# Placing the split weights at thirteen small distances inside their buffers, with fourteen activation slots in place of fifteen

## The chip, the core and the metric

The kernel runs on one core of one Trainium2 chip. The metric is the device time of one execution in microseconds (us). Two runs of the kernel before took 3163.54 and 3163.57 us; their median is 3163.56 us.

## The reference, cut to what matters

Two transformer-like blocks work one after the other on 256 tokens of width 2048, all in float32. Nearly all the arithmetic is a chain of matrix products with large weights, and the rest (norms, two kinds of attention in the first block; a state space branch "s5", a gated linear attention "gla" and a differential attention "diff" in the second) hangs between them:

```python
proj = h @ w_in[i]                                   # first block, 10240 columns
merged = (jax.nn.sigmoid(gate_sb) * (y_sb @ w_sb_out[i])
          + jax.nn.sigmoid(gate_ca) * (y_ca @ w_ca_out[i]))
x = x + merged @ w_mix_out[i]
g_ff, u_ff = jnp.split(h @ w_ffn_in[i], 2, axis=-1)
x = x + (jax.nn.silu(g_ff) * u_ff) @ w_ffn_out[i]
...
proj = hn @ w_in[l]                                  # second block
y_a = s5_branch(u_ssm, ...)
y_b = gla_branch(q_gla, k_gla, v_gla, ...)
y_c = diff_attn_branch(q_diff, k_diff, v_diff, ...)
h = h + merged.astype(h.dtype) @ w_out[l]
h = h + conv_gated_mlp(rmsnorm_2(h, norm_ffn_w[l]), ffn_w_up[l], ...)
```

## The kernel before, in words

**Products in parts.** Each float32 operand is split into a high part (rounded to the type float32r) and a low part (the rest), and a product is the sum of high x high, high x low and low x high. Activations lie in "slots" `s` as blocks of 128 rows (the contraction) by 512 numbers: 256 high parts, then 256 low parts. Weights come as tiles `raw` of 128x1024 ("halves"), loaded by SyncE (L460); ScalarE makes the high part `wh` (L467, `high`) and VectorE the low part `wl` (L477, `low`).

**Jobs.** The list of jobs is walked by `stream`, half by half. There are three kinds. In an AS job (100 of them) the weights are the moving operand: 128x512 of `wh` or `wl` stream past a 128x128 block of activations that was loaded as the stationary operand (L561, L562, L563). In a WS job (123 of them) it is the other way round: a 128x128 block of `wh` or `wl` is the stationary operand, and 512 columns of activations stream past the high block (L527), 256 past the low block (L531); a job is 32 such pairs in four halves of eight. One job is of a third kind, W4. Each job adds up in one of two PSUM buffers `acc`, and its "evac" generator empties `acc` when the last half is through.

**What sets the order.** Everything is issued in the order in which `stream` writes it, each engine running its own instructions in that order and waiting on semaphores. Before the matmuls of half i, the high split of half i+4 and the low split of half i+3 are issued; there are four `raw`, five `wh` and four `wl` buffers. After each half `tick()` advances every waiting generator by one step, and so heads, norms and evacuations are woven between the halves: a step's results have one half's time to become ready. A generator that wants a slot (`gslot`) and finds none free yields, and tries again at the next tick. A job whose `acc` buffer is still held by the job two before it forces ticks without matmuls in between (`self.tick(must=True)`), and so do `drain` and a half whose activations are not ready.

**Slots.** There are `NSLOT = 15` slots of 8192 bytes per partition; they hold activations, values, keys, a head's working space and more. The second block's heads take them in the stretch of the jobs `w_vd`, `w_u`, `w_qkd`: there `slotfree` is empty at many ticks. A gla head (`gla_head`) takes a slot `s` and then a slot `s3` for its running state: VectorE copies the first step (L1117) and adds the next six (L313), and TensorE reads them (L1130, L1134); `head_norm` follows (square on ScalarE at L310, a sum on TensorE at L1382). The evac of a `w_qkd` job (`ws_keep`, `ws_sum`) takes a slot for every four jobs and fills it from `acc` (copy on ScalarE L442, add on VectorE L443).

**Addresses.** In the built program every slot and every `raw`, `wh` and `wl` buffer starts at a multiple of 128 bytes within the partition, and every block of 128 or 512 numbers of them that TensorE reads too. The tile `big`, which is transposed at L346, lies 64 bytes past such a multiple.

Of the kernel before, what the change touches and what calls it, by code (L numbers as in the profile page):

```python
# [10 lines left out]
F32R = mybir.dt.float32r  # L11
# [12 lines left out]
CA = 4  # L24
SA = 3
COOL = 1
RAWB = 4


# [23 lines left out]
def _as(w):  # L53

    K, N = w.shape
    if K % 256:
        w = np.concatenate([w, np.zeros((256 - K % 256, N), w.dtype)], axis=0)
        K = w.shape[0]
    return np.ascontiguousarray(
        w.reshape(K // 256, 2, 128, N // 512, 512).transpose(3, 0, 2, 1, 4).reshape(-1, 128, 1024))  # L60

# [122 lines left out]


class Build:
    NSLOT = 15

    def __init__(self, tc, d, out, es):
        self.tc, self.nc, self.d, self.out = tc, tc.nc, d, out  # L190
        pool = lambda name, bufs, **kw: es.enter_context(tc.tile_pool(name=name, bufs=bufs, **kw))
        self.slotp, self.one = pool("slots", 1), pool("one", 1)
        self.rawp, self.whp, self.wlp = pool("raw", RAWB), pool("wh", CA + 1), pool("wl", SA + 1)
        self.ev = pool("ev", 2)
# [3 lines left out]
        self.psfree, self.cooling, self.ticks = [0, 1, 2, 3], [], 0  # L198
        self.slotfree = list(range(self.NSLOT))
        self.gens, self.lanes, self.nm = [], {}, 0  # L200
# [44 lines left out]
    def unbank(self, b):  # L245
        self.cooling.append((self.ticks + COOL, b[1]))

# [201 lines left out]
    def stream(self, jobs):  # L449
        nc = self.nc  # L450
        halves = [(j, i, ks) for j in jobs for i, ks in j.halves]
        N = len(halves)
        raws, spl = {}, {}
        width = lambda j, ks: {"AS": 512 * len(ks), "WS": 1024, "W4": 512}[j.kind]

        def load(i):
            j, idx, ks = halves[i]
            n = width(j, ks)
            r = self.rawp.tile([128, 1024], F32, tag="raw", name=self.name("raw"))
            nc.sync.dma_start(out=r[:, :n], in_=self.d[j.w][idx][:, :n])  # L460
            raws[i] = r

        def high(i):
            j, idx, ks = halves[i]
            n = width(j, ks)
            wh = self.whp.tile([128, 1024], F32R, tag="wh", name=self.name("wh"))
            nc.scalar.copy(wh[:, :n] if j.kind != "W4" else wh[:, :n].bitcast(F32), raws[i][:, :n])  # L467
            spl[i] = wh

        def low(i):  # L470
            j, idx, ks = halves[i]
            n = width(j, ks)
            r, wh = raws.pop(i), spl[i]
            wl = None
            if j.kind != "W4":
                wl = self.wlp.tile([128, 1024], F32R, tag="wl", name=self.name("wl"))
                nc.vector.tensor_sub(wl[:, :n], r[:, :n], wh[:, :n].bitcast(F32))  # L477
            spl[i] = (wh, wl)
            if i + RAWB < N:
                load(i + RAWB)  # L480

        ahead = self.at_start(load)
        for i in range(CA):
            next(ahead)
            high(i)
            if i < SA:
                low(i)
        self.add(ahead)
        last, prev, acc = None, None, None
        for i, (j, idx, ks) in enumerate(halves):  # L490
            if i + CA < N:
                high(i + CA)
            if i + SA < N:
                low(i + SA)
            if j is not last:
                if j.before is not None:
                    j.before()
                while prev is not None and not prev.free:
                    self.tick(must=True)
                prev, last = last, j  # L500
                acc = self.accp.tile([128, 2, 512], F32, tag="acc", name=self.name("acc"))
            for k in ks:
                while k not in j.acts.ready:
                    self.tick(must=True)
            first, end = j.halves[0][1][0], j.halves[-1][1][-1]
            if j.by_m is not None:

                for m in range(2):
                    for q, (_, _, kq) in enumerate(halves[i:]):
                        self.mm_as(j.acts, kq, *spl[i + q], acc, (m,), first, end)  # L510
                    j.by_m(m, acc)
                break
            wh, wl = spl.pop(i)
            if j.kind == "AS":
                self.mm_as(j.acts, ks, wh, wl, acc, (0, 1), first, end, low_last=i == 0)
            elif j.kind == "W4":

                for k in range(16):
                    p = slice(32 * (k % 4), 32 * (k % 4) + 32)
                    nc.tensor.matmul(acc[p, 0, :], lhsT=wh[:, 32 * k:32 * k + 32].bitcast(F32),  # L520
                                     rhs=j.acts.at(k).bitcast(F32), start=k < 4, stop=k >= 12)
            else:
                for kk, k in enumerate(ks):
                    x = j.acts.at(k)
                    for f in range(2):
                        s = slice((kk * 2 + f) * 128, (kk * 2 + f) * 128 + 128)
                        hi = lambda: nc.tensor.matmul(  # L527
                            acc[:, f, :], lhsT=wh[:, s], rhs=x, start=k == first, stop=k == end)
                        if k == first:
                            hi()  # L530
                        nc.tensor.matmul(acc[:, f, 256:512], lhsT=wl[:, s], rhs=x[:, 0:256], start=False, stop=False)  # L531
                        if k != first:
                            hi()
            if i + 1 == N or halves[i + 1][0] is not j:
                self.add(j.evac(acc, lambda j=j: setattr(j, "free", True)), front=True)
            self.tick()
        while self.gens:
            self.tick(must=True)
# [63 lines left out]
    def first(self):  # L602
# [6 lines left out]
        def start(load):  # L609
# [4 lines left out]
            def load_xt(g):  # L614
                nc.sync.dma_start(out=xs[g // 4][0][:, (g % 4) * 2:(g % 4) * 2 + 2], in_=d["xt"][:, 2 * g:2 * g + 2])

            for g in range(RAWB):
                load_xt(g)
                load(g)
            for k in range(16):  # L620
                if k % 2 == 0 and k // 2 + RAWB < 8:
                    load_xt(k // 2 + RAWB)
                if k == 8:
# [1146 lines left out]
```

## Time and profile before

| | |
|---|---|
| median of the two runs | 3163.56 us |
| the profiled execution's own time | 3164.05 us |
| its span | 3162.2 us |
| TensorE matmul busy | 3143.5 us, 16909 instructions |
| TensorE weight load busy | 2669.4 us |
| VectorE busy | 1993.3 us |
| ScalarE busy | 1553.2 us |
| granted TensorE clock, mean | 0.999 |

The page names TensorE's matmuls PE and its weight loads PEld, VectorE DVE, ScalarE ACT, GpSimd POOL and SyncE SP. A group's line has the line of the kernel, the engine, the operation, output<-inputs, the shape and the count; behind the first bar the busy time in us and the mean duration of one in ns; behind the second the idle time of that engine just before these instructions and what ended it. Matmuls are pipelined, so a matmul of 398 ns may start 227 ns after the one before it: what a matmul costs in a dense row is the distance from start to start, which the timeline gives (its columns are start in us, duration in us, engine, line, operation).

### The profile page before, as it was taken

The numbers are of one execution on the slowest core, as the hardware profiler recorded it, in microseconds if no ns is written. First come the engines' busy times: TensorE is split into PE (matmuls) and PEld (weight loads), VectorE is DVE, ScalarE is ACT, GpSimd is POOL, SyncE is SP. The second block draws the span as 40 slices with busy tenths as digits, with TensorE's granted clock in tenths as the row PEclk, the third lists the DMA queues.
The fourth block names the chain that finished last, engine by engine and source line by source line (L and its number), as shares of the span: only waits on it lengthen the run. The fifth ranks groups of instructions, "written<-read, shape, count | busy, mean of one in ns | idle before, by whom it ended". The sixth has DMA issues, their size and how long they took to land.

```text
span 3162.2 us, 43735 instructions
## 1 busy us (share of the span) xinstructions
PE 3143.5 (99%) x16909; PEld 2669.4 (84%) x16909; DVE 1993.3 (63%) x2593; ACT 1553.2 (49%) x2035; POOL 72.5 (2%) x158
## 2 busy tenths in 40 slices
PE   8999999999999999999999999999999999999998
PEld 7888888888888888888888888888888888888887
DVE  5656445557576676566655667945555766757666
ACT  6544444455444454456544454434445644545545
POOL 0000000000001000000000001000000000000000
PEclk9999999999999999999999999999999999999999
DMA  7455555555667666555654565655555565565555
GB/s 263 169 179 167 187 193 187 187 185 187 212 222 246 244 223 240 183 176 197 212 177 159 170 215 193 213 186 199 199 187 186 181 195 187 186 198 183 191 187 166
DMA packets 172640, 617.90 MB, mean 195 GB/s; under 512 B 23553, under 2 KB 23969, under 8 KB 169233
## 3 DMA queue, kind: packets, MB, share of 16 engines
q1 hardware_dynamic: 164992, 577.49, 55.1%
q0 software_dynamic: 7440, 37.64, 3.5%
q8 instruction: 132, 2.16, 0.3%
q14 instruction: 76, 0.61, 0.1%
HBM read 599.74 MB, written 14.25 MB: 194 GB/s over the span
## 4 chain that ended last, share of the span: by engine, by line
PE 99%; ACT 0%; DMA 0%; DVE 0%; DVEq 0%; issue 0%; SPq 0%; ACTq 0%
PE acc L527 29%; PE acc L561 17%; PE acc L563 17%; PE acc L562 17%; PE acc L531 15%; PE p L346 1%; PE p L1675 0%; PE p L1134 0%; PE p L1715 0%; PE p L908 0%; PE p L910 0%; PE p L909 0%; PE p L1718 0%; PE p L1111 0%; PE p L1130 0%; PE p L1709 0%
## 5 line engine op out<-in xcount | busy, mean ns | idle before, releaser
L477 DVE TENSOR_TENSOR wl<-raw,wh 128x1024 fp32r<-128x1024 f32 x1088 | 1320.2, 1220 | 649.9 <-PE acc L562 428.8
L467 ACT CAST wh<-raw 128x1024 fp32r<-128x1024 f32 x1088 | 1139.5, 1050 | 1092.5 <-PE acc L563 657.2
L527 PE MATMUL acc<-s,wh 128*128 128x512 f32 x3936 | 1385.2, 398 | 0.0
L531 PE MATMUL acc<-s,wl 128*128 128x256 f32 x3936 | 1090.7, 282 | 0.0
L561 PE MATMUL acc<-wh,s 128*128 128x512 f32 x2372 | 933.3, 393 | 0.8 <-DVE big L1353 0.8
L563 PE MATMUL acc<-wh,s 128*128 128x512 f32 x2372 | 925.0, 390 | 0.0
L562 PE MATMUL acc<-wl,s 128*128 128x512 f32 x2372 | 924.5, 390 | 0.0
L527 PEld LDWEIGHTS acc<-s,wh 128*128 128x128 f32 x3936 | 735.6, 188 | 165.0
L531 PEld LDWEIGHTS acc<-s,wl 128*128 128x128 f32 x3936 | 744.6, 189 | 11.0 <-issue 1.0
L561 PEld LDWEIGHTS acc<-wh,s 128*128 128x128 f32 x2372 | 446.0, 188 | 92.6 <-issue 1.7
L563 PEld LDWEIGHTS acc<-wh,s 128*128 128x128 f32 x2372 | 445.6, 188 | 92.9
L562 PEld LDWEIGHTS acc<-wl,s 128*128 128x128 f32 x2372 | 446.1, 188 | 91.0 <-issue 0.5
L443 DVE TENSOR_TENSOR s<-acc,s 128x512 f32<-128x512 f32 (+1 forms) x120 | 82.7, 690 | 273.9 <-ACT s L442 273.9
L442 ACT COPY s<-acc 128x512 f32<-128x512 f32 (+1 forms) x120 | 70.1, 584 | 196.6 <-PE acc L527 194.6
L310 ACT ACTIVATE s<-s 128x256 f32<-128x256 f32 (+4 forms) x175 | 76.6, 443 | 105.1 <-DVE s L313 38.2
L313 DVE SCALAR_TENSOR_TENSOR s<-s,conv 128x256 f32<-128x256 f32 x172 | 79.4, 482 | 3.4 <-ACT s L310 0.3
L445 DVE TENSOR_TENSOR s<-s,rb 128x512 f32<-128x512 f32 (+1 forms) x104 | 71.7, 690 | 3.5
L318 ACT CAST s<-s 128x256 fp32r<-128x256 f32 (+1 forms) x104 | 45.5, 441 | 30.4 <-DVE s L948 15.3
L1632 DVE TENSOR_TENSOR s<-s,s 128x1024 f32<-128x1024 f32 x48 | 58.5, 1219 | 0.0
L310 ACT ACTIVATE s<-s,conv 128x256 f32<-128x256 f32 x86 | 47.1, 595 | 22.0 <-DVE s L445 22.0
L319 DVE TENSOR_TENSOR s<-s,s 128x256 fp32r<-128x256 f32 (+1 forms) x104 | 47.5, 459 | 13.8 <-ACT s L318 12.5
L310 ACT ACTIVATE junk<-big 128x512 f32<-128x512 f32 x48 | 30.3, 632 | 49.5 <-DVE big L927 35.1
(265 smaller groups left out, 1036.8 us busy)
## 6 DMA issues: line engine op xcount, KB each, us to landing
raw<-in_w_fin SPq DMA_DIRECT2D x176, 512.0 KB, 4.3
raw<-in_w_up SPq DMA_DIRECT2D x172, 512.0 KB, 3.8
raw<-in_w_fout SPq DMA_DIRECT2D x88, 512.0 KB, 4.3
raw<-in_w_down SPq DMA_DIRECT2D x84, 512.0 KB, 4.1
raw<-in_w_qksb SPq DMA_DIRECT2D x32, 512.0 KB, 3.5
raw<-in_w_qkca SPq DMA_DIRECT2D x32, 512.0 KB, 3.3
raw<-in_w_gsb SPq DMA_DIRECT2D x32, 512.0 KB, 3.3
raw<-in_w_gca SPq DMA_DIRECT2D x32, 512.0 KB, 4.2
```

Source lines behind the costliest of these rows:

```text
L310: self.nc.scalar.activation(out, in_, func, scale=scale, **kw)
L313: self.nc.vector.scalar_tensor_tensor(out=out, in0=in0, scalar=scalar, in1=in1, op0=op0, op1=op1)
L442: nc.scalar.copy(out, acc[:, 0:n, 256:512])
L443: nc.vector.tensor_add(out, acc[:, 0:n, 0:256], out)
L445: nc.vector.tensor_mul(out, out, rb.tile[:, None, :].to_broadcast([128, n, 256]) if n > 1 else rb.tile[:, None, :])
L467: nc.scalar.copy(wh[:, :n] if j.kind != "W4" else wh[:, :n].bitcast(F32), raws[i][:, :n])
L477: nc.vector.tensor_sub(wl[:, :n], r[:, :n], wh[:, :n].bitcast(F32))
L527: hi = lambda: nc.tensor.matmul(acc[:, f, :], lhsT=wh[:, s], rhs=x, start=k == first, stop=k == end)
L531: nc.tensor.matmul(acc[:, f, 256:512], lhsT=wl[:, s], rhs=x[:, 0:256], start=False, stop=False)
L561: nc.tensor.matmul(acc[:, m, :], lhsT=xl, rhs=wh[:, s], start=k == first, stop=False)
L562: nc.tensor.matmul(acc[:, m, :], lhsT=xh, rhs=wl[:, s], start=False, stop=False)
L563: nc.tensor.matmul(acc[:, m, :], lhsT=xh, rhs=wh[:, s], start=False, stop=k == end)
```

## The change

The buffers `wh` and `wl` become 1152 numbers wide in place of 1024, and a job's weights start `o` numbers into them. `o` is taken in turn from a list of thirteen, separately counted for each kind of job: 0, 4, 8, 16, 24, 32, 40, 48, 64, 80, 96, 112 and 128 bytes. The nine buffers grow by 4608 bytes per partition in all, and `NSLOT` goes from 15 to 14, which takes 8192 bytes away.

```diff
+PLACES = (0, 1, 2, 4, 6, 8, 10, 12, 16, 20, 24, 28, 32)
...
 class Build:
-    NSLOT = 15
+    NSLOT = 14
...
+        place, count = {}, {}
+        for j in jobs:
+            place[id(j)] = count[j.kind] = count.get(j.kind, -1) + 1
...
         def high(i):
             j, idx, ks = halves[i]
             n = width(j, ks)
-            wh = self.whp.tile([128, 1024], F32R, tag="wh", name=self.name("wh"))
+            o = PLACES[place[id(j)] % len(PLACES)]
+            wh = self.whp.tile([128, 1024 + 128], F32R, tag="wh", name=self.name("wh"))[:, o:o + 1024]
...
             if j.kind != "W4":
-                wl = self.wlp.tile([128, 1024], F32R, tag="wl", name=self.name("wl"))
+                o = PLACES[place[id(j)] % len(PLACES)]
+                wl = self.wlp.tile([128, 1024 + 128], F32R, tag="wl", name=self.name("wl"))[:, o:o + 1024]
```

In the built program of the change the buffers still start at multiples of 128 bytes, 4608 bytes apart, so `o` alone sets where the weights stand against such a multiple. Of the 7128 matmuls whose moving operand is `wh` or `wl`, 588 start 4 bytes past a multiple of 8 bytes, and 2406 off a multiple of 16 bytes (places 4, 8, 24 and 40); of the 7872 stationary blocks of the WS jobs, 640 and 2496. Activations stay at multiples of 128 bytes. No instruction is added or removed in the weights' path.

The one slot fewer moves instructions, and only in the second block's heads. In the change the evac of the first `w_qkd` job finds no slot, holds its `acc`, and the third `w_qkd` job forces six ticks; before, no tick was forced there. At the first `w_gluv` job three ticks are forced, before it was one. Line numbers of the change are higher by five or six than those of before from the class on.

TensorE, the start of the third `w_qkd` job, before. `acc_14631` is the second job's sum, `acc_14745` the third's; `p_14696` is the last gla head's output, of which these rows make the second half; the first half of it stands eight pairs earlier.

```order
L531 MATMUL acc_14631<-s_12510,wl_14627 128x256
L527 MATMUL acc_14631<-s_12510,wh_14598 128x512
L1130 MATMUL p_14696<-s_13702,s_13082 128x128
L1134 MATMUL p_14696<-s_13702,s_13820 128x32 x3
L1130 MATMUL p_14696<-s_13702,s_13082 128x128
L1134 MATMUL p_14696<-s_13702,s_13820 128x32 x4
L527 MATMUL acc_14745<-s_11905,wh_14625 128x512
L531 MATMUL acc_14745<-s_11905,wl_14653 128x256
```

Half of a head's output stands between the two jobs. The same place in the change, where `acc_14604` is the second job's sum, `acc_14744` the third's, `p_14715` the last gla head's output and `s_14527` its running state:

```order
L533 MATMUL acc_14604<-s_12510,wh_14574 128x512
L1136 MATMUL p_14715<-s_14259,s_13082 128x128
L1140 MATMUL p_14715<-s_14259,s_14527 128x32 x3
L1136 MATMUL p_14715<-s_14259,s_13082 128x128
L1140 MATMUL p_14715<-s_14259,s_14527 128x32 x4
L1136 MATMUL p_14715<-s_14259,s_13082 128x128
L1140 MATMUL p_14715<-s_14259,s_14527 128x32 x3
L1136 MATMUL p_14715<-s_14259,s_13082 128x128
L1140 MATMUL p_14715<-s_14259,s_14527 128x32 x4
L533 MATMUL acc_14744<-s_11905,wh_14598 128x512
```

Both halves of the head's output now stand together between two jobs, with no weight matmuls between them. VectorE at the same place, before (the running state is `s_13820`):

```order
L1117 COPY s_13820<-p_14563 128x256
L313 SCALAR_TENSOR_TENSOR s_13820<-s_13820,s_13702,p_14564 128x256
L477 TENSOR_TENSOR wl_14600<-raw_14484,wh_14574 128x1024
L443 TENSOR_TENSOR s_14620<-acc_14515,s_14620 128x512
L313 SCALAR_TENSOR_TENSOR s_13820<-s_13820,s_13702,p_14565 128x256
L313 SCALAR_TENSOR_TENSOR s_13820<-s_13820,s_13702,p_14566 128x256
L477 TENSOR_TENSOR wl_14627<-raw_14513,wh_14598 128x1024
```

And in the change (the running state is `s_14527`; `wl_14708` is the low part for the third half after the one that is waited for; `acc_14510` is the first `w_qkd` job's sum):

```order
L483 TENSOR_TENSOR wl_14684<-raw_14578,wh_14658 128x1024
L314 SCALAR_TENSOR_TENSOR s_14527<-s_14527,s_14259,p_14649 128x256
L314 SCALAR_TENSOR_TENSOR s_14527<-s_14527,s_14259,p_14650 128x256
L483 TENSOR_TENSOR wl_14708<-raw_14602,wh_14682 128x1024
L314 SCALAR_TENSOR_TENSOR s_14527<-s_14527,s_14259,p_14647 128x256
L314 SCALAR_TENSOR_TENSOR s_14527<-s_14527,s_14259,p_14648 128x256
L314 SCALAR_TENSOR_TENSOR s_14527<-s_14527,s_14259,p_14649 128x256
L314 SCALAR_TENSOR_TENSOR s_13702<-s_13702,par,s_12583 128x256 x2
L320 TENSOR_TENSOR s_14734<-s_13702,s_14734 128x2x256
L444 TENSOR_TENSOR s_14740<-acc_14510,s_14740 128x512
```

The last three steps of the state, which had low splits of later halves between them, now follow each other; the first `w_qkd` job's sum is emptied behind them, where before it stood ahead of them.

## The prediction, made before the changed kernel was run

> **What bounds the kernel now.** I read the page's busy times first, then the shares of the chain that ended last, then who waited on TensorE.
>
> ```profile
> span 3162.2 us, 43735 instructions
> PE 3143.5 (99%) x16909; PEld 2669.4 (84%) x16909; DVE 1993.3 (63%) x2593; ACT 1553.2 (49%) x2035; POOL 72.5 (2%) x158
> ...
> PE 99%; ACT 0%; DMA 0%; DVE 0%; DVEq 0%; issue 0%; SPq 0%; ACTq 0%
> PE acc L527 29%; PE acc L561 17%; PE acc L563 17%; PE acc L562 17%; PE acc L531 15%; PE p L346 1%; PE p L1675 0%; PE p L1134 0%; PE p L1715 0%; PE p L908 0%; PE p L910 0%; PE p L909 0%; PE p L1718 0%; PE p L1111 0%; PE p L1130 0%; PE p L1709 0%
> ```
>
> ```profile
> PE acc L553 <- ACT wh L467: 8.4, 1, 8.4
> PE acc L561 <- DVE big L1353: 0.8, 1, 0.8
> ```
>
> TensorE is the chain, 99% of it, and over the whole span it waits 9.2 us for others: 8.4 at the start and 0.8 near the end. So the time is the number of matmuls times the distance from one start to the next, and the two questions on the change are whether that distance depends on where the weights start, and whether the slot that is gone makes TensorE wait. The distances are in the timeline of TensorE. First an AS job, first and last row with 40 matmuls between them; then a usual WS job and a quicker one, each with 24 pairs between the two rows.
>
> ```profile
> 1500.14 0.39 PE L561 MATMUL acc<-wh,s 128*128 128x512 f32 x1
> ...
> 1509.43 0.39 PE L563 MATMUL acc<-wh,s 128*128 128x512 f32 x1
> ```
>
> ```profile
> 1183.30 0.40 PE L527 MATMUL acc<-s,wh 128*128 128x512 f32 x1
> ...
> 1191.77 0.40 PE L527 MATMUL acc<-s,wh 128*128 128x512 f32 x1
> ```
>
> ```profile
> 1172.20 0.39 PE L527 MATMUL acc<-s,wh 128*128 128x512 f32 x1
> ...
> 1180.52 0.39 PE L527 MATMUL acc<-s,wh 128*128 128x512 f32 x1
> ```
>
> AS: 9.29 us over 41 steps, 0.2266 us a matmul. WS: 8.47 / 24 = 0.353 us a pair, and in some jobs 8.32 / 24 = 0.347 us. The jobs differ in nothing but the moment at which they begin, so a WS pair, in which two weight loads must fit, settles into one of a few rhythms. The counts are these:
>
> ```profile
> L527 PE MATMUL acc<-s,wh 128*128 128x512 f32 x3936 | 1385.2, 398 | 0.0
> L531 PE MATMUL acc<-s,wl 128*128 128x256 f32 x3936 | 1090.7, 282 | 0.0
> L561 PE MATMUL acc<-wh,s 128*128 128x512 f32 x2372 | 933.3, 393 | 0.8 <-DVE big L1353 0.8
> L563 PE MATMUL acc<-wh,s 128*128 128x512 f32 x2372 | 925.0, 390 | 0.0
> L562 PE MATMUL acc<-wl,s 128*128 128x512 f32 x2372 | 924.5, 390 | 0.0
> ```
>
> 7116 x 0.2266 = 1612 us, 3936 x 0.353 = 1389 us: 3001 of the 3162 us are matmuls with a weight operand that the change moves. One nanosecond on each of them would be 15 us.
>
> **The change part by part.**
>
> *The splits write at the new places* (ACT L467, DVE L477), and neither sets the end. Whether they get slower has a row: the evacuation of the feed-forward jobs is the same instruction in both blocks, but in the second block its output starts 8 bytes further on in rows of 1032 bytes. The groups by line and shape, 950 to 1450 us (first block), then 2300 to 3100 us (second):
>
> ```profile
> L443 DVE TENSOR_TENSOR s<-acc,s 128x512 f32<-128x512 f32 x25 | 17.3, 692 | 56.1 <-ACT s L442 56.1
> L442 ACT COPY s<-acc 128x512 f32<-128x512 f32 x25 | 14.6, 586 | 37.2 <-PE acc L527 37.2
> ```
>
> ```profile
> L443 DVE TENSOR_TENSOR s<-acc,s 128x512 f32<-128x512 f32 x41 | 28.4, 692 | 99.1 <-ACT s L442 99.1
> L442 ACT COPY s<-acc 128x512 f32<-128x512 f32 x41 | 24.0, 586 | 71.8 <-PE acc L527 71.8
> ```
>
> 692 and 692 ns, 586 and 586 ns: no cost. The cover, should 4 bytes differ, is the matmuls of one half: 12 x 0.227 = 2.72 us in AS, 8 x 0.353 = 2.82 us in WS, against the splits:
>
> ```profile
> L477 DVE TENSOR_TENSOR wl<-raw,wh 128x1024 fp32r<-128x1024 f32 x1088 | 1320.2, 1220 | 649.9 <-PE acc L562 428.8
> L467 ACT CAST wh<-raw 128x1024 fp32r<-128x1024 f32 x1088 | 1139.5, 1050 | 1092.5 <-PE acc L563 657.2
> ```
>
> Even at twice 1.22 us the low split fits, and it waits mostly for TensorE to give a buffer back. Without that cover, doubling it for the jobs at 4 bytes (one in thirteen of 1088 halves) would be 84 x 1.22 = 102 us of VectorE time. I take 0.
>
> *TensorE reads from the new places.* No row of before has a TensorE operand off a multiple of 32 bytes. The nearest is the transposes: the block that they load as stationary lies 64 bytes past a multiple of 128 in `big`, and on one in the slots.
>
> ```profile
> L346 PEld LDWEIGHTS p<-cst,big 128*128 128x128 f32 x128 | 15.0, 141 | 2.0
> L346 PEld LDWEIGHTS p<-cst,s 128*128 128x128 f32 x64 | 7.1, 140 | 1.6 <-DVE s L800 1.1
> ```
>
> 141 against 140 ns: a 64-byte shift costs a load nothing, and the finer places are open. Bounds for the AS matmuls: below, the gain of the second rival; above, the loss of the first. For the WS pairs there is a narrower pair as well, if only the rhythm is shifted: all in the quick one, 3936 x (0.347 - 0.353) = -24 us; as much the other way, +24 us, is an estimate by symmetry. I take 0, by the row with the 64-byte shift, which is the nearest, and because the AS step shows no trace of the buffer: 41 steps of 12 to a half run through four `wh` and four `wl` buffers, and through both 2048-byte parts of each, at one even pace.
>
> *One slot fewer.* At the third `w_qkd` job the ticks are forced, and TensorE has nothing else to run. In the order, what it now waits for is: the low split L477 of a later half, which cannot begin before TensorE has finished the last half of the job (its buffer is that half's), 1.22 us; behind it on VectorE the last three steps of the state; then, with the head's output done, the square on ScalarE, the copy of the first `w_qkd` job's sum and the add that frees `acc`.
>
> ```profile
> L313 DVE SCALAR_TENSOR_TENSOR s<-s,s,p 128x256 f32<-128x256 f32 x24 | 11.5, 478 | 0.7
> L310 ACT ACTIVATE s<-p 128x512 f32<-128x512 f32 x10 | 6.0, 596 | 2.8 <-PE p L1134 1.7 <-PE p L910 1.1
> L1134 PE MATMUL p<-s,s 128*128 128x32 f32 x112 | 13.9, 265 | 0.0
> L1130 PE MATMUL p<-s,s 128*128 128x128 f32 x32 | 6.8, 295 | 0.0
> ```
>
> 1.22 + 3 x 0.478 = 2.65 us, of which TensorE covers 1.2 us with the first quarter of the head's output (its first two and six of these passes, 2 x 6.8 / 32 + 6 x 13.9 / 112): 1.5 us. Then 0.596 + 0.586 + 0.692 = 1.87 us with nothing beside it. [...] Together 3.9 us. What is queued behind: on ScalarE the next high splits, of which four are already done, on SyncE two `raw` loads that now stand behind the small transfers of s5, issued four halves (11 us) ahead of their use. At the first `w_gluv` job three ticks are forced for one; the s5 output has two halves of that job (5.4 us) before its second group is needed, so I add 1 us and no more. POOL's four bias instructions move past loads of s5 and are not waited for. Sum: +5 us, between 0 (if the heads' earlier steps ran ahead) and +12 (both places at twice the estimate).
>
> **Sum.** 3164.05 us is the profiled execution, 1.85 us of it outside the span, and 0.5 us above the median. On the median: 3163.6 + 0 (splits) + 0 (reads) + 5 (waits) = 3169 us.
>
> **The rivals.** *A start inside a line costs reads (slower).* If TensorE takes its numbers in larger pieces and a start off a piece splits them, then the 588 AS matmuls at odd multiples of 4 bytes would pay, and of the WS jobs 320 pairs, in which a stationary block at such a place loads during the 256-column matmul. At twice the step the price is 588 x 0.227 = 133 us, and 320 x 0.141 = 45 us by the load's duration, so 178 us: 3347 us. At half of it, one piece in two split, 89 us: 3258 us. It decides from 15 us over 588 matmuls, 25 ns each, where it would be seen beside the rest; from 63 us (2%), 107 ns each, it changes the verdict. For it: nothing in the trace lies at 4 bytes. Against it: VectorE and ScalarE writes that start 8 bytes off show nothing. [...]
>
> *Equal starts are what slows the reads now (faster).* All operands of these matmuls begin on multiples of 128 bytes, so the two streams of TensorE could be meeting in the same place. What a 512-column pass costs without that has one hint: a plain float32 product, of two passes, followed by one AS matmul.
>
> ```profile
> 1565.14 1.02 PE L1040 MATMUL p<-s 128*128 128x512 f32 x2
> 1565.59 0.80 PE L561 MATMUL acc<-wh,s 128*128 128x512 f32 x1
> 1566.23 0.40 PE L562 MATMUL acc<-wl,s 128*128 128x512 f32 x1
> ```
>
> From 1565.14 to 1566.23 are 1.09 us; less 0.227, 0.43 us a pass. If such a pass takes two column times, half of it is 0.215 us, 12 ns under the AS step. Eleven of the thirteen places are no multiple of 128 bytes: 11/13 x 7116 x 0.012 = -72 us, 3097 us with the waits; and with the WS pairs at 0.215 + 0.108, 11/13 x 3936 x 0.030 = -100 us more, 2997 us. Against it: the two streams differ in length, one 512 numbers and one 128, so they drift apart, and yet the AS step is the same throughout; a fixed cost per matmul, or per number, does that as well. [...]
>
> *The waits are larger.* The slot that is gone would have to cost 63 us to matter; eight more forced ticks, at a half's 2.8 us each, are 22 us. That stays within 2%, and I count it with the forecast.
>
> **How the numbers follow.** Forecast, the reads as before and some microseconds of waits: 0.77, 3169 us, by itself 3140 (waits 0, quick rhythm) to 3200 (waits 12, slow rhythm). Slower by the first rival: 0.15. Faster by the second: 0.08. A measurement of this kernel tells from no change about 2%, 63 us, which is 3100 to 3227; all of the forecast lies within. For the range I keep the forecast's bounds and reach part of the way to the cheap end of the first rival, since a loss on the AS matmuls alone (half of 133 us) would give 3235 us: 3140 to 3235 us, with the rest of both rivals, 2 in 10, left out. Faster 0.08, same 0.77, slower 0.15.
>
> **What would show it.** Right: the AS step stays at 0.2266 us in every job and WS pairs at 0.347 to 0.36 us, whatever the place; TensorE's waits on VectorE and ScalarE grow by about 5 us between 1750 and 1860 us; L467 and L477 stay at 1050 and 1220 ns. Wrong: a step that changes from job to job with a period of thirteen jobs of a kind. If only one job in thirteen is slow, the first rival holds; if all but two are quicker, the second. If TensorE waits more than 12 us in the middle of the kernel, the slot was mis-sized.

## The result, and the profile after

The changed kernel takes 3202.29 us (median of 3201.75 and 3202.83), the kernel before 3163.56 us: a ratio of 1.0122 with a 95% interval of 1.0079 to 1.0166. That lies inside the predicted range of 3140 to 3235 us and within 2% of before, but 33 us above the predicted 3169 us. The profiled execution is the one of 3201.75 us. Its page first: span, busy times, and the chain's shares by engine.

```profile
span 3199.7 us, 43739 instructions
PE 3178.0 (99%) x16909; PEld 2670.1 (83%) x16909; DVE 1994.0 (62%) x2593; ACT 1548.9 (48%) x2033; POOL 73.0 (2%) x158
...
PE 99%; DVE 0%; ACT 0%; DMA 0%; issue 0%; DVEq 0%; SPq 0%; ACTq 0%
```

TensorE is still the whole chain: the same 16909 matmuls, and 34.5 us more of busy time (3143.5 before). So nothing else has become the bound; the matmuls themselves have moved apart. Who TensorE waits for:

```profile
PE acc L559 <- ACT wh L472: 8.1, 1, 8.1
PE acc L533 <- DVE s L444: 2.9, 1, 2.9
PE acc L567 <- DVE big L1359: 0.8, 1, 0.8
PE p L1140 <- DVE s L314: 0.3, 1, 0.3
```

Two waits are new, 2.9 and 0.3 us, both at the third `w_qkd` job. That is 3.2 us of the 37.5 us by which the span has grown. The rest is in the groups by line:

```profile
L483 DVE TENSOR_TENSOR wl<-raw,wh 128x1024 fp32r<-128x1024 f32 x1088 | 1320.8, 1220 | 686.4 <-PE acc L568 472.9
L472 ACT CAST wh<-raw 128x1024 fp32r<-128x1024 f32 x1088 | 1136.9, 1048 | 1129.5 <-PE acc L569 685.7
L533 PE MATMUL acc<-s,wh 128*128 128x512 f32 x3936 | 1381.2, 396 | 2.9 <-DVE s L444 2.9
...
L567 PE MATMUL acc<-wh,s 128*128 128x512 f32 x2372 | 943.8, 398 | 0.8 <-DVE big L1359 0.8
L568 PE MATMUL acc<-wl,s 128*128 128x512 f32 x2372 | 935.4, 394 | 0.0
L569 PE MATMUL acc<-wh,s 128*128 128x512 f32 x2372 | 935.2, 394 | 0.0
```

The splits write as fast as before (1220 ns, and 1048 against 1050). The three AS lines are 4 to 5 ns longer (393, 390, 390 before), the WS line 2 ns shorter (398 before). But the matmuls overlap: in the rows below they last 0.39 to 0.40 us, and their starts are 0.23 to 0.24 us apart. So the step from start to start decides. Three AS jobs that follow each other, in TensorE's timeline, two rows of each with 41 steps from the first to the second; their weights lie at 128, 0 and 4 bytes:

```profile
831.27 0.40 PE L567 MATMUL acc<-wh,s 128*128 128x512 f32 x1
...
840.80 0.39 PE L569 MATMUL acc<-wh,s 128*128 128x512 f32 x1
...
847.95 0.39 PE L567 MATMUL acc<-wh,s 128*128 128x512 f32 x1
...
857.24 0.39 PE L569 MATMUL acc<-wh,s 128*128 128x512 f32 x1
...
864.49 0.40 PE L567 MATMUL acc<-wh,s 128*128 128x512 f32 x1
...
874.24 0.40 PE L569 MATMUL acc<-wh,s 128*128 128x512 f32 x1
```

9.53 / 41 = 0.2324 us at 128 bytes, 9.29 / 41 = 0.2266 at 0 bytes, 9.75 / 41 = 0.2378 at 4 bytes. The same reading over all jobs of the changed kernel, with the addresses of the built program beside the start times (AS: mean step of a job in ns; WS: the time of a pair that most jobs at that place show, both where two occur):

```
place, bytes     0    4    8   16   24   32   40   48   64   80   96  112  128
AS step      227.7 237.6 233.6 231.7 233.4 233.2 233.4 233.3 229.2 231.1 233.4 230.5 232.4
WS pair   347/353 350.2 347/349 346.6 346.6 353.3 353.3 346.6 353.4 353.3 346.6 353.3 350.9
```

Before, all AS jobs stood at 227.0 on average. Added up from start to start, AS matmuls took 1631.8 us before and 1668.9 now (+37.1), WS matmuls 1395.5 and 1391.7 (-3.8), all others with the waits behind them 116.6 and 121.3 (+4.7): +38.0 us, against 37.7 us between the two profiled executions' own times. So nearly the whole loss is the AS step, and it is paid at every place but 0.

In the built program of before, every weight block that an AS matmul streams and every activation block that it loads start 128 bytes past a multiple of 256. The first theory, "distance" (called "phase" in the first expectations): the step hangs on how far the two operands' starts are apart, modulo some power of two. Its rivals: "line" (only where the weights themselves start counts) and "slot" (the loss comes from the fourteen slots).

### The profile page after: what moved, and what is told of

Same layout as the page of the kernel before. It is cut to its first block, busy times and chain, and to the rows that moved or that the text cites. A ratio compares the mean times of both kernels' runs of the same rounds, so it can differ in the third digit from the quotient of the medians.

```text
span 3199.7 us, 43739 instructions
## 1 busy us (share of the span) xinstructions
PE 3178.0 (99%) x16909; PEld 2670.1 (83%) x16909; DVE 1994.0 (62%) x2593; ACT 1548.9 (48%) x2033; POOL 73.0 (2%) x158
## 4 chain that ended last, share of the span: by engine, by line
PE 99%; DVE 0%; ACT 0%; DMA 0%; issue 0%; DVEq 0%; SPq 0%; ACTq 0%
PE acc L533 29%; PE acc L567 17%; PE acc L569 17%; PE acc L568 17%; PE acc L537 15%; PE p L347 1%; PE p L1681 0%; PE p L1140 0%; PE p L1721 0%; PE p L915 0%; PE p L916 0%; PE p L914 0%; PE p L1724 0%; PE p L1117 0%; PE p L1715 0%; PE p L1136 0%
## 5 line engine op out<-in xcount | busy, mean ns | idle before, releaser
L483 DVE TENSOR_TENSOR wl<-raw,wh 128x1024 fp32r<-128x1024 f32 x1088 | 1320.8, 1220 | 686.4 <-PE acc L568 472.9
L472 ACT CAST wh<-raw 128x1024 fp32r<-128x1024 f32 x1088 | 1136.9, 1048 | 1129.5 <-PE acc L569 685.7
L567 PE MATMUL acc<-wh,s 128*128 128x512 f32 x2372 | 943.8, 398 | 0.8 <-DVE big L1359 0.8
L568 PE MATMUL acc<-wl,s 128*128 128x512 f32 x2372 | 935.4, 394 | 0.0
L569 PE MATMUL acc<-wh,s 128*128 128x512 f32 x2372 | 935.2, 394 | 0.0
L569 PEld LDWEIGHTS acc<-wh,s 128*128 128x128 f32 x2372 | 446.3, 188 | 105.4
L567 PEld LDWEIGHTS acc<-wh,s 128*128 128x128 f32 x2372 | 446.2, 188 | 104.4 <-issue 1.6
L568 PEld LDWEIGHTS acc<-wl,s 128*128 128x128 f32 x2372 | 446.5, 188 | 102.2 <-issue 0.5
L319 ACT CAST s<-s 128x256 fp32r<-128x256 f32 (+1 forms) x104 | 45.5, 441 | 27.8 <-DVE s L954 15.2
L320 DVE TENSOR_TENSOR s<-s,s 128x256 fp32r<-128x256 f32 (+1 forms) x104 | 47.3, 457 | 13.9 <-ACT s L319 13.9
L981 DVE TENSOR_TENSOR big<-big,acc 128x1024 f32<-128x1024 f32 x24 | 29.3, 1221 | 41.6 <-PE acc L569 41.6
```

Source lines behind the costliest of these rows:

```text
L567: nc.tensor.matmul(acc[:, m, :], lhsT=xl, rhs=wh[:, s], start=k == first, stop=False)
L568: nc.tensor.matmul(acc[:, m, :], lhsT=xh, rhs=wl[:, s], start=False, stop=False)
L569: nc.tensor.matmul(acc[:, m, :], lhsT=xh, rhs=wh[:, s], start=False, stop=k == end)
```

## The experiments

**One slot fewer alone.** Fourteen slots and wide buffers, all weights at 0 bytes.

```diff
-PLACES = (0, 1, 2, 4, 6, 8, 10, 12, 16, 20, 24, 28, 32)
+PLACES = (0,)
```

> The change with every place at 0: fourteen slots and the wider buffers, but no shift. Theory 'phase' (the distance between the start of TensorE's moving and stationary operand sets the step) and theory 'line' (the weights' own start, against some multiple, sets it): AS step back at 0.2268 us, only the wait at the third w_qkd job left, 3163.6 + 4 = 3168 us, within 2. Theory 'slot' (the missing slot and the wider buffers made the loss): 3195 to 3202 us.

3170.69 us, ratio 1.0022 (1.0013 to 1.0031) to before, so 6.7 us for the slot. The AS jobs are back at 227.0 ns on average, and the WS pairs have before's mean of 352.9. "Slot" as the main cause falls: 31.6 of the 38.7 us come from the places. What the 6.7 us are is in TensorE's timeline at the third `w_qkd` job (in front the last head's output, `p`) and in the granted clock by windows:

```profile
1787.86 1.65 PE L1140 MATMUL p<-s,s 128*128 128x32 f32 x8
1792.43 0.77 PE L533 MATMUL acc<-s,wh 128*128 128x512 f32 x1 [2.92 <-DVE s L444]
...
1794.07 0.63 PE L533 MATMUL acc<-s,wh 128*128 128x512 f32 x1
...
1797.27 0.63 PE L533 MATMUL acc<-s,wh 128*128 128x512 f32 x1
...
1798.40 0.40 PE L533 MATMUL acc<-s,wh 128*128 128x512 f32 x1
1798.63 0.28 PE L537 MATMUL acc<-s,wl 128*128 128x256 f32 x1
```

```profile
1784.56:1787.97 3.41, 2.92 (x23) 1.00 0.49 169
1787.97:1798.21 10.24, 7.32 (x27) 0.50 0.28 102
1798.21:1808.00 9.79, 9.79 (x57) 1.00 0.50 162
```

A row of the windows gives the stretch, its length, TensorE's busy time and count, the granted clock, then the transfers' share and GB/s. The wait is 2.92 us; behind it five pairs take 1797.27 - 1794.07 = 3.20 us, 0.64 each in place of 0.353, because the granted clock has fallen: it is 0.50 from 1787.97 to 1798.21 us. The wait did not start this. It begins at 1792.43 - 2.92 = 1789.51 us, 1.5 us after the fall, which comes while TensorE is at the small matmuls of the head's output. Before, with weight matmuls between the halves of that output, the clock was 1.00 throughout this stretch. In the changed kernel the half clock lasts 6.83 us here (1804.79 to 1811.62) and not 10.24, with the same wait of 2.92 us. Against before, the sums from start to start are +5.3 us for the other matmuls (3.2 of it the two waits), +3.1 for WS and -0.7 for AS. So the waits are less than half of the price, and the fallen clock makes most of the rest.

**All weights at 128 bytes; and everything at 128 bytes.** The second kernel puts an unused piece of 128 bytes ahead of the slots, so activations and weights move together.

```diff
+PLACES = (32,)
```

```diff
+PLACES = (0,)
...
+        pool("pad", 1).tile([128, 32], F32, tag="pad", name="pad")
         self.slotp, self.one = pool("slots", 1), pool("one", 1)
```

> The change with every place at 128 bytes, so weights at multiples of 128 but 128 bytes nearer to the activations' start modulo 512. Theories 'phase' and 'line' (with a multiple over 128): AS step 0.2324 us and WS pair 0.351 us as in the change's jobs at that place, 3163.6 + 4 + 7116 x 0.0056 - 3936 x 0.002 = 3200 us. A line of 128 bytes or less: 3168 us, as with no shift.

> Every place at 0, and 128 bytes left free ahead of the slots, so that activations and weights all move on by 128 bytes together. Theory 'phase': nothing changes against the kernel without shift, AS step 0.2268 us, 3168 us. Theory 'line': the weights start where they start with the place 128, so AS step 0.2324 us, WS pair 0.351 us, 3200 us.

The weights alone: 3206.12 us, 1.0132 (1.0115 to 1.0149). Everything: 3170.72 us, 1.0022 (1.0012 to 1.0031), the time of one slot fewer alone. The same job in both, first and last of 42 rows; first the weights alone, then everything (the added line makes L567 to L569 L568 to L570):

```profile
832.57 0.39 PE L567 MATMUL acc<-wh,s 128*128 128x512 f32 x1
...
842.10 0.39 PE L569 MATMUL acc<-wh,s 128*128 128x512 f32 x1
```

```profile
819.86 0.39 PE L568 MATMUL acc<-wh,s 128*128 128x512 f32 x1
...
829.16 0.39 PE L570 MATMUL acc<-wh,s 128*128 128x512 f32 x1
```

9.53 against 9.30 us, 232.4 against 226.8 ns, with the weights at the same residue modulo 512 (the same remainder of their start divided by 512) in both. "Line" falls: where the weights start makes no difference as long as the activations start likewise.

**The activations alone.** The piece of 128 bytes ahead of the slots moves everything; 384 bytes more bring the weights back to the residue that they had before.

```diff
+PLACES = (96,)
...
+        pool("pad", 1).tile([128, 32], F32, tag="pad", name="pad")
         self.slotp, self.one = pool("slots", 1), pool("one", 1)
```

> The weights keep the starts that they had before, modulo 512 bytes; only the activations' slots lie 128 bytes further on. Theory 'distance': every AS step is 232.4 ns as with the weights alone moved by 128 bytes, and the time is 3206 us (3200 to 3210). Rival 'weights' starts' (what counts is where the weights themselves lie): AS steps of 227.0 ns and 3171 us, the time of one slot fewer alone.

3205.5 us in one run, as "distance" has it. The same job:

```profile
832.18 0.39 PE L568 MATMUL acc<-wh,s 128*128 128x512 f32 x1
...
841.71 0.39 PE L570 MATMUL acc<-wh,s 128*128 128x512 f32 x1
```

9.53 us over 41 steps again. The weights are written, and streamed, at the same residues as with one slot fewer alone; the slots have moved by 128 bytes, and with them all other buffers. So a clash of TensorE's stream with the splits that write the weights does not explain the step either. Nor does other work beside the stream, as the trace of the kernel with all weights at 128 bytes shows: 1651 of its AS steps fall where VectorE, ScalarE and GpSimd are idle, and they take 232.5 ns on average, the 5231 others 232.4; 117 fall where no DMA transfer runs either, and they take 232.8. It is TensorE's own two operands that matter (226.8 ns with both moved by 128 bytes, 232.4 with either alone).

**A scan from 0 to 512 bytes.** Steps of 16 bytes, in turn by jobs.

```diff
+PLACES = tuple(range(0, 129, 4))
```

> Thirty-three places from 0 to 512 bytes in steps of 16, in turn by jobs; the step is read job by job from the trace. Both theories: 0.2268 us at 0 and at 512 bytes if the period is 512 or a part of it, the known 0.229 to 0.2335 us at 16 to 128. Theory 'phase' says nothing of which places between 128 and 512 are quick, but that there are quick ones and none under 0.2266 us; whole time 3190 to 3205 us. If the AS step at some place lies under 0.222 us, the 0.2266 us of the kernel before is itself a cost of placement.

3201.23 us in one run. AS jobs at 256, 64 and 384 bytes, each first and last of 42 rows:

```profile
2424.90 0.39 PE L567 MATMUL acc<-wh,s 128*128 128x512 f32 x1
...
2434.19 0.39 PE L569 MATMUL acc<-wh,s 128*128 128x512 f32 x1
...
2218.52 0.39 PE L567 MATMUL acc<-wh,s 128*128 128x512 f32 x1
...
2227.91 0.39 PE L569 MATMUL acc<-wh,s 128*128 128x512 f32 x1
...
813.94 0.39 PE L567 MATMUL acc<-wh,s 128*128 128x512 f32 x1
...
823.47 0.40 PE L569 MATMUL acc<-wh,s 128*128 128x512 f32 x1
```

9.29 at 256 bytes, 9.39 at 64, 9.53 at 384 (128 past 256): 226.6, 229.0 and 232.4 ns. The mean AS steps of the three jobs at each place (at 0 those at 512 too), in ns:

```
bytes        0    16    32    48    64    80    96   112   128   144   160   176   192   208   224   240
+0       227.3 231.6 233.3 232.1 229.3 231.1 233.6 231.1 232.4 232.9 234.2 232.2 233.2 234.8 233.2 235.1
+256     227.0 231.6 233.3 233.2 230.5 231.1 233.5 231.1 232.6 233.2 234.2 232.6 233.2 234.6 233.2 232.3
```

The two rows agree within 1.2 ns but for the last column, where one of the three jobs at 496 bytes ran at 226.9 and the others at 233.6 and 236.4. So the period is 256 bytes, and no place is quicker than 0; one job at 496 bytes met the quick step.

**All weights at 4 bytes.** The prediction's first rival at its strongest.

```diff
+PLACES = (1,)
```

> All weights 4 bytes further on, in every job. By the steps of the changed kernel's jobs at 4 bytes (AS 237.6 ns, WS pairs 350.2): 7128 AS matmuls by 10.6 ns = 75.6 us, 3944 WS pairs by -2.7 ns = -10.6 us, on top of 3170.7 us: 3236 us (3225 to 3245), slower than before by over 2%. The prediction's first rival at its own price (half a step more wherever a start lies inside a line): 7128 by 113 ns on the AS jobs alone, 3970 us or more.

3238.37 us in one run, slower than before by 2.4%. The mean AS step, read as above, is 237.6 ns, and every job lies between 236.6 and 238.0. The jobs of the changed kernel foretold this kernel within 2.4 us (3236 expected): a job's step belongs to its own place and not to its neighbours'. And 4 bytes cost 11 ns a matmul, not the half step of 113 that the rival would have.

**Places by kind of job.** AS at 0; WS (and W4) at 16 bytes, where nearly all WS pairs had been quick.

```diff
-PLACES = (0, 1, 2, 4, 6, 8, 10, 12, 16, 20, 24, 28, 32)
+PLACES = {"AS": 0, "WS": 4, "W4": 4}
...
+            o = PLACES[j.kind]
```

> The AS jobs' weights stay at place 0, those of the WS jobs and of the W4 job lie 16 bytes further on in every job; 14 slots. Theory 'distance' (a matmul's step hangs on the distance of the two operands' starts, taken modulo 256 bytes): AS steps 227.0 ns as at place 0, WS pairs 346.6 ns as at place 16 bytes in the kernels with many places, in every WS job, where they took 352.9 ns on average with one slot fewer alone. 3170.7 us less 3944 pairs by 6.3 ns = 25 us: 3146 us (3142 to 3150), faster than before by 0.5%. Rival 'neighbours' (a job's rhythm comes from the places of the jobs before and after it, and the mean over thirteen places only looks like a price of each): the WS pairs spread between 346.6 and 353.4 as they did, 3158 to 3171 us.

3153.5 us, ratio 0.9969 (0.9958 to 0.9981): quicker than both kernels, by 10 us than before and by 49 than the change, in spite of the slot. A WS job of it, 24 pairs from the first row to the last:

```profile
1177.75 0.39 PE L533 MATMUL acc<-s,wh 128*128 128x512 f32 x1
...
1186.07 0.39 PE L533 MATMUL acc<-s,wh 128*128 128x512 f32 x1
```

8.32 / 24 = 0.347 us; with one slot fewer alone this job took 0.353 a pair, as the usual one before. But the expected 3146 was missed by 7.5 us. By the pairs that nothing interrupts, 98 of the 123 WS jobs fell, by 6.6 ns a pair on average. The other 25 had been quick with one slot fewer alone already, most of them jobs whose pairs stand between the matmuls of heads. Nine pairs of such a job, there, with its weights at 0 bytes:

```profile
100.88 0.39 PE L533 MATMUL acc<-s,wh 128*128 128x512 f32 x1
...
104.00 0.40 PE L533 MATMUL acc<-s,wh 128*128 128x512 f32 x1
```

3.12 / 9 = 0.347 us. I had counted 6.3 ns on all jobs, and on the first pairs of each too, before the rhythm settles. From start to start WS went from 1398.6 to 1381.4 us, -17.2, which is the gain measured (3170.7 to 3153.5). "Neighbours" falls too: with 16 bytes everywhere all jobs settle at 347 to 349 ns.

**The slot given back in part.** Buffers 256 bytes longer and not 512, and in the room a shorter fifteenth piece for the gla heads.

```diff
+        self.ev, self.short = pool("ev", 2), pool("short", 1)
...
+            if self.shortfree:
+                self.shortfree = False
+                s = self.short.tile([128, 1288], F32, tag="short", name=self.name("s")), "short"
+            else:
+                s = yield from self.gslot([128, 2048])
+            cum, ki, E, qd, sc = (s[0][:, i * 256:i * 256 + 256] for i in range(5))
+            kt = E
```

> As the kernel with places by kind, but the weights' buffers are 256 bytes longer and not 512, and the room left holds a fifteenth, shorter piece (1288 numbers a row) for the gla heads, whose own table is drawn together (the product with the decay is written over the decay). Theory: of TensorE's two waits (2.9 us on VectorE at the third w_qkd job and 0.3 us) most of the first goes, and with it the clock's fall behind it, 6.7 us together; AS 227.0 ns and WS 346.6 ns stay. 3146 less 5 to 6.7: 3140 us (3137 to 3145). Rival: the wait comes from the work before it (the gla heads end no earlier) and not from the slot; then 3146 us, with a gap of 2.5 to 3.5 us still there near 1790 us.

3154.52 us, 0.997 (0.9959 to 0.9981): no gain over places by kind alone. TensorE's waits, without the first one at the start, and its timeline behind the second row's wait (AS lines L570 to L572 here):

```profile
PE acc L571 <- DVE wl L486: 2.1, 1, 2.1
PE acc L536 <- DVE s L447: 1.4, 1, 1.4
```

```profile
1975.35 0.39 PE L570 MATMUL acc<-wh,s 128*128 128x512 f32 x1
1977.85 0.50 PE L571 MATMUL acc<-wl,s 128*128 128x512 f32 x1 [2.11 <-DVE wl L486]
...
1979.97 0.63 PE L572 MATMUL acc<-wh,s 128*128 128x512 f32 x1
1980.40 0.63 PE L570 MATMUL acc<-wh,s 128*128 128x512 f32 x1
```

The old wait shrank from 2.9 to 1.4 us and the one of 0.3 went. A new one of 2.1 us came 200 us later, and behind it the AS step is 0.43 us for a while, at a granted clock of 0.50 for 3.41 us. VectorE's timeline ahead of it:

```profile
1968.16 0.69 DVE L1403 TENSOR_TENSOR s<-p,s 128x512 f32<-128x512 f32 x1 [4.79 <-ACT s L314]
...
1970.12 0.69 DVE L1403 TENSOR_TENSOR s<-p,s 128x512 f32<-128x512 f32 x1 [0.94 <-ACT s L314]
...
1976.58 1.22 DVE L486 TENSOR_TENSOR wl<-raw,wh 128x1024 fp32r<-128x1024 f32 x1
```

VectorE waits 4.79 us for ScalarE, then does the last steps of two heads one behind the other (L1403 twice), and the low split that TensorE needs, L486, stands behind both. From start to start, against places by kind alone, the other matmuls took 2.6 us less and the AS matmuls 5.1 us more. That the slot makes the wait holds in part: with the shorter piece half of it went, and 1.4 us stayed. That the cost would vanish does not hold. The new wait came with this edit, but no run here takes apart which piece of the edit brought it. The period is borne out once more: with the shorter buffers 3100 of the 7128 AS matmuls have operands whose starts are 256 bytes nearer modulo 512, and the AS step is 227.0 ns as before.

## Why the prediction was right, and where it was wrong

The measured 3202.29 us lies in the stated range by luck. The forecast's own bounds were 3140 to 3200 us; only the part of the range that was added for the first rival reaches further, and the runs speak against that rival's mechanism. The sign that was named for being wrong is there too: the AS step changes from job to job with the place, and neither of the two patterns that were foreseen for it came.

*Splits at new places, 0 us*: right (1220 and 1048 ns).

*Reads from new places, 0 us*: wrong, and the step that failed. That the place of the weights costs TensorE nothing was read from rows in which no distance changed; the runs show an AS step that hangs on the distance of the two operands' starts modulo 256 bytes (in the changed kernel 227.7 ns at 0 bytes and 229.2 to 237.6 at the other places). The loss is +37.8 us on the AS matmuls and -6.9 on WS, the changed kernel against one slot fewer alone. The ground given was that the AS step shows no trace of the buffer, through eight buffers and both 2048-byte parts of each. The observation was true, but in all of them the two operands' starts are a multiple of 256 bytes apart, so these rows did not vary what the change varies. The other ground, a load that lies 64 bytes off and is no longer (141 against 140 ns), was a duration of one instruction beside a question on the step between two.

*The first rival, a start inside a line*: the sign was right, the mechanism not. It was to show as one dear job in thirteen; in fact eleven of the twelve places other than 0 cost 2 to 7 ns (229.2 to 233.6 against 227.0) and 4 bytes 11. At most the 4 ns by which 4 bytes lie above the next place (237.6 against 233.6) could be what the rival meant; no other odd multiple of 4 bytes was run. Nor does it order the steps whether a start is a multiple of 16 bytes: 32 and 128 bytes, which are, take 233.2 and 232.4 ns, and 8, 24 and 40, which are not, 233.6, 233.4 and 233.4.

*The second rival, equal starts slow the reads*: the reverse of what was found. Equal starts modulo 256 bytes are the best place for AS (227.3 and 227.0 ns in the scan), and no place of the scan came near the 215 ns of that rival's estimate.

*The WS bounds, -24 to +24 us by rhythm*: they held (-6.9 for the thirteen places, -17.2 at 16 bytes throughout; about 1 us of each, by an estimate from the slow pairs, is the half clock, which lasted 6.83 us there and 10.24 with one slot fewer alone). But the rhythm is not set by the moment at which a job begins alone, as the prediction had it. At 16 bytes all jobs settle in the quick one (347 to 349 ns); at 0 bytes 98 settle at 353 ns, and 25, most of them interrupted by other matmuls, in the quick one.

*Waits, +5 us*: 6.7 us with one slot fewer alone. The place was right: 3.2 us of waiting at the third `w_qkd` job, where 3.9 were predicted, and none at `w_gluv`, where 1 was. The parts of the 3.9 were not. Of the 1.5 us ahead of the head's output 0.3 showed; behind it 2.9 us showed for 2.4, because ScalarE's L319 (0.62 us) and VectorE's L320 (0.69) stand before the copy, where the sum had the square of 0.6. The two errors nearly cancel. The 2.4 holds 0.5 us for five hand-overs between engines, a term that no run shows; in the changed kernel the wait of 2.92 us, less the four instructions in it (0.62, 0.69, 0.59 and 0.69), leaves 0.33 us for them. That 5 came near 6.7 us is owed to a term that was not in the sum: the granted clock falls to 0.50 around the wait, and the pairs take 0.64 us for a while. It came without a long wait ahead of it: waits of 2.1 and 1.4 us in the last kernel were each followed by it, and with one slot fewer alone it came after 3.41 us in which TensorE was busy for 2.92 with small matmuls.

What remains open: why the step depends on this distance. The runs show that it takes both operands (tried at 128 bytes), that the period is 256 bytes, and that at equal starts the AS steps, uneven at first, settle on 226, 227, 227 ns, while at other places they settle on other cycles (229, 232, 226 at 64 bytes; 230, 235, 235 or 234, 233, 233 at 8). How the chip comes to this, no run here tests; whether the matmuls would be evenly quick without loads between them wasn't tried.

## What to carry to other kernels

"No dependence in the trace" counts only for what the trace varies: before an even pace is taken as proof, look up whether the addresses that the change moves differ in it at all. Where TensorE is the bound, look at starts and not at durations, for each kind of job apart; streamed and loaded operands whose starts agree modulo 256 bytes suited the weight-streaming jobs here (227.0 ns a step), 16 bytes of difference the weight-loading ones (0.347 us a pair). The second was worth 17 us of 3171; 4 bytes for all weights cost 68. Around a wait of TensorE look at the granted clock as well: with one slot fewer alone, 3.2 us of waiting came with 10.24 us at half clock, and with a loss of 6.7 us.

## What the runs showed of the hardware that was not expected

The AS step takes values from 226.6 ns (at 0 bytes) to 237.8 (at 4 bytes) by nothing but the distance of two start addresses, in kernel after kernel. The WS pair takes mostly 346.6 or 353.4 ns, with 349 to 351 at 4, 128 and some places beyond, in no order of the distance that I can see. And the granted clock fell after a wait of only 1.4 us, in the last kernel; the timeline of TensorE, and the clock (1.00, then 0.50) by windows:

```profile
1780.15 0.50 PE L536 MATMUL acc<-s,wh 128*128 128x512 f32 x1 [1.40 <-DVE s L447]
...
1781.61 0.63 PE L536 MATMUL acc<-s,wh 128*128 128x512 f32 x1
...
1782.25 0.63 PE L536 MATMUL acc<-s,wh 128*128 128x512 f32 x1
```

```profile
1777.76:1781.17 3.41, 2.01 (x16) 1.00 0.44 154
1781.17:1784.58 3.41, 3.41 (x12) 0.50 0.86 308
```

The wait ends at 1780.15 us; the clock falls 1 us later, at 1781.17, and the pairs of 0.64 us come then, not at once. Apart from the start and the end of the program, the half clock came in stretches of 3.41 us (twice in this kernel), 6.83 (in the changed one) and 10.24 (with one slot fewer alone): once, twice and three times the first.
